# Layer-norm deviations kept on chip, another order of operand splits, and an output projection that reads its last operands last

## The chip, the cores and the metric

The kernel runs on one core of a Trainium2 chip. The metric is device time in microseconds (us), the median of several executions. Engines run in parallel and each runs its own instructions in program order: PE (matmul) with its weight loads (PEld), DVE and ACT (elementwise), POOL, and SP, which here only issues transfers. ACT and POOL issue transfers too. Semaphores hold an instruction until what it needs is there.

## What is computed

One encoder block on x of 1024 positions by 1024 channels, float32. Two mixers read the same normalised input, their gated sum goes through an output projection, and a gated MLP with a convolution follows.

```python
def conformer_conv(a, g, dw_w, dw_b, ln_g, ln_b):
    h = a * jax.nn.sigmoid(g)
    h = depthwise_conv(h, dw_w, dw_b)
    h = layer_norm(h, ln_g, ln_b)
    return jax.nn.silu(h)

n = rms_norm(h, norm1_g[l])
z = n @ w_in[l]
z_u, z_v, z_a, z_g, z_ga, z_gb = jnp.split(z, split_at, axis=-1)
y_a = spatial_gating(jax.nn.gelu(z_u), jax.nn.gelu(z_v), ...) @ w_a_out[l]
y_b = conformer_conv(z_a, z_g, ...) @ w_b_out[l]
merged = jax.nn.sigmoid(z_ga) * y_a + jax.nn.sigmoid(z_gb) * y_b
h = h + merged @ w_o[l]
n = rms_norm(h, norm2_g[l])
gate, val = jnp.split(n @ w_up[l], 2, axis=-1)
gate = depthwise_conv(gate, ffn_dw_w[l], ffn_dw_b[l])
h = h + (jax.nn.gelu(gate) * val) @ w_down[l]
out = rms_norm(h, final_g)
```

## The kernel before

Activations are held transposed, 128 channels by 1024 positions a tile (512 KB). Every operand of a matmul is split by `split` into a rounded high part (a cast by ACT) and a low part (a subtraction by DVE), and a product of two operands is three matmuls: high x high, high x low, low x high. `mm_both` does this for one output tile: for each of eight operand blocks k, six matmuls of 128 x 512, so 48 for an output.

Order of the program: the input projections (u, v, a, g, then the gates ga and gb), the products with w_a and w_b, the output projection with w_o, the MLP. While the gate projections run on PE, the layer norm of the convolution (`conv_norm`) is done in the background: `fill` takes steps off the list `bg` according to a planner's clock, `PE.now`, which adds up assumed costs. Its steps: `mean` (sum of the channels by two matmuls), eight `dev` (load a tile from DRAM, subtract the mean, store it to DRAM, square it, add the square to `csum`), `var` and `var2` (reciprocal standard deviation, broadcast), eight `fin` (load the deviations again, multiply, Silu). After each second `fin`, `c_sums` makes four sums and differences of the pair, which POOL stores to `fb_d`; from there the operands of the convolution's units are read.

The products with w_a and w_b are done by `strassen`: eight units (`ab_units`; 0 to 3 are branch A with w_a, 4 to 7 branch B with w_b), each with seven products (1 to 7) of half size, instead of eight. A unit wants weight sums. `Unit` lets POOL make them by accumulating transfers while loading; `SumUnit` loads the weights once and lets DVE add. The operand blocks of unit 0 are loaded and split by `s_blocks` and prepared in the last three gate projections (`prepare`); within a unit, `slot` after each product hands out the next splits and loads. Between two products a copy by ACT (L659, L666, L671, L676) moves a half bank; the products 1, 3, 5 and 6 among others stand behind such copies.

`Merged` fetches the merged branch (`merged_d`) in unit 7 and splits its first six tiles; the last two, from unit 7 itself, are multiplied, added and split by `direct` at its end. Then the output projection: for each output j a load of x, a weight from `W.get()` (which also splits up to two further weights ahead), 48 matmuls, `evac_o` (addition to x by DVE, a square by ACT, a sum by DVE, for each half) and a store to `h_d`.

Pools: `ap` gives 16 slots of 8 KB a partition, tag a8, to the eight normalised activations, the split operand blocks and some weights; `wp` gives 3 slots to weights; `sp` gives 15 slots of 4 KB to everything else. A tile that takes a slot waits until the last reader of the slot's tile before is through. There are four banks of the matmul's output.

## Time and profile before

| | |
|---|---|
| executions | 1505.01, 4063.05, 1500.4 us; median 1505.01 |
| profiled execution | 1502.72 us, span 1500.9 us, mean granted clock of PE 0.989 |
| PE | 1460.4 us busy, 97% |
| PEld | 1211.4 us, 81% |
| DVE | 1027.2 us, 68% |
| ACT | 630.3 us, 42% |
| POOL | 144.5 us, 10% |

A view of the trace gives either totals (the page, the waits) or rows in order of time (the timeline): where a row says "[7.70 <-ACT w L130]", its engine sat idle for 7.70 us before, until an instruction of ACT at line 130 that writes a tile w. The granted clock of PE is a share of 2.4 GHz; 0.50 is 1.2 GHz.

### The profile page before, as it was taken

Reading aid. Unit: us, or ns where it says so; the run is one execution under the profiler, and the core shown is the slowest. Engines: PE = TensorE matmul, PEld = TensorE weight load, DVE = VectorE, ACT = ScalarE, POOL = GpSimd, SP = SyncE. Lnnn points to the kernel's source line nnn. Section 1 sums busy time; section 2 is a strip of 40 time slices with the busy share of each in tenths; the row PEclk is TensorE's granted clock in tenths of the full one; section 3 lists DMA queues with packets and bytes.
Section 4 is the critical chain, followed back from the end, with each engine's and each line's share of the span. In section 5 each row is a group of like instructions: output and inputs, shape, how many; then the busy total and the mean of one; then the engine's idle time right before and its main releaser. Section 6 shows DMA issues by size and latency. Waiting matters only on the chain.

```text
span 1500.9 us, 17240 instructions
## 1 busy us (share of the span) xinstructions
PE 1460.4 (97%) x6634; PEld 1211.4 (81%) x6634; DVE 1027.2 (68%) x1085; ACT 630.3 (42%) x769; POOL 144.5 (10%) x180
## 2 busy tenths in 40 slices
PE   9999999999999996999999999999999999999998
PEld 7888888888888875878788888888888887878887
DVE  6899989888999746595644875555555448464545
ACT  6433244343422555363323454444444447363353
POOL 0000000000000011000000012111111111112000
PEclk9999999999999997999999999999999999999999
DMA  5343575445614788577444289777777779999743
GB/s 202 98 96 100 157 196 150 119 134 160 164 62 154 270 299 327 183 285 235 139 155 141 72 223 262 201 200 198 199 196 198 187 186 296 282 369 289 254 174 113
DMA packets 108770, 289.70 MB, mean 193 GB/s; under 512 B 10640, under 2 KB 12944, under 8 KB 108688
## 3 DMA queue, kind: packets, MB, share of 16 engines
q1 hardware_dynamic: 76032, 207.85, 40.0%
q0 software_dynamic: 24000, 57.68, 19.7%
q10 hardware_dynamic: 8656, 23.08, 4.0%
q8 instruction: 52, 0.85, 0.2%
q14 instruction: 30, 0.25, 0.1%
HBM read 185.80 MB, written 73.40 MB: 173 GB/s over the span
## 4 chain that ended last, share of the span: by engine, by line
PE 79%; DVE 9%; DMA 5%; issue 3%; ACT 3%; SPq 1%; ACTq 0%; DVEq 0%; POOLq 0%
PE bank L69 79%; DVE s L69 7%; DMA s<-fb_d 2%; DVE a L69 2%; DMA s<-in_w_down 1%; DMA fb_d<-s 1%; ACT a L130 1%; DMA h_d<-s 1%; DVE w L69 0%; DMA s<-in_xT 0%; DMA s<-h_d 0%; ACT w L130 0%; ACT s L792 0%; SPq L539 0%; DVE hb L69 0%
## 5 line engine op out<-in xcount | busy, mean ns | idle before, releaser
L69 PE MATMUL bank<-a,w 128*128 128x512 f32 (+1 forms) x4146 | 952.9, 389 | 24.9 <-ACT w L130 8.6
L69 PEld LDWEIGHTS bank<-a,w 128*128 128x128 f32 x4146 | 773.1, 189 | 190.6 <-ACT w L130 9.4
L69 PE MATMUL bank<-a,a 128*128 128x512 f32 (+2 forms) x1934 | 419.0, 374 | 7.1 <-ACT s L671 6.2
L69 PEld LDWEIGHTS bank<-a,a 128*128 128x128 f32 x1934 | 344.3, 189 | 73.5 <-ACT s L671 7.1
L69 DVE TENSOR_TENSOR w<-s,w 128x1024 fp32r<-128x1024 f32 (+3 forms) x144 | 162.0, 1127 | 222.9 <-ACT w L130 215.9
L69 DVE TENSOR_TENSOR a<-s,a 128x1024 fp32r<-128x1024 f32 (+2 forms) x186 | 198.5, 1093 | 134.8 <-ACT a L130 134.4
L69 DVE SCALAR_TENSOR_TENSOR s<-hb,vt,s 128x1024 f32<-128x1024 f32 x204 | 248.2, 1277 | 0.0
L130 ACT CAST w<-s 128x1024 fp32r<-128x1024 f32 (+2 forms) x143 | 138.8, 973 | 136.6 <-PE bank L69 88.2
L130 ACT CAST a<-s 128x1024 fp32r<-128x1024 f32 (+2 forms) x142 | 138.7, 996 | 66.8 <-DVE s L69 19.2
L69 DVE TENSOR_TENSOR s<-s,bank 128x1024 f32<-128x1024 f32 (+2 forms) x128 | 110.4, 881 | 36.2 <-PE bank L69 25.4
L69 DVE TENSOR_TENSOR s<-s,s 128x1024 f32<-128x1024 f32 (+1 forms) x98 | 95.4, 980 | 10.4 <-ACT s L780 7.9
L69 PE MATMUL bank<-w,a 128*128 128x512 f32 x384 | 87.2, 389 | 0.0
L69 PEld LDWEIGHTS bank<-w,a 128*128 128x128 f32 x384 | 72.1, 188 | 15.0
L586 POOL DMA_DIRECT2D s<-s x56 | 49.4, 882 | 269.5 <-DMA s<-in_w_up 87.2
L586 POOL DMA_DIRECT2D s<-in_w_up x40 | 41.1, 1028 | 266.3 <-DMA s<-in_w_up 243.9
L69 DVE TENSOR_TENSOR csum<-csum,s 128x1024 f32<-128x1024 f32 (+2 forms) x55 | 45.7, 831 | 22.4 <-ACT s L1432 11.2
L676 ACT ACTIVATE s<-bank 128x512 f32<-128x512 f32 x36 | 21.5, 598 | 93.9 <-PE bank L69 93.8
L446 POOL DMA_DIRECT2D s<-s x28 | 24.3, 866 | 371.0 <-ACT s L445 309.2
L659 ACT COPY bank<-bank 128x512 f32<-128x512 f32 x36 | 20.6, 571 | 67.2 <-PE bank L69 66.8
L671 ACT ACTIVATE s<-bank 128x512 f32<-128x512 f32 x36 | 21.5, 597 | 60.3 <-PE bank L69 57.6
L931 ACT ACTIVATE s<-bank 128x1024 f32<-128x1024 f32 x16 | 16.4, 1025 | 69.7 <-PE bank L69 62.0
L1220 ACT ACTIVATE s<-s 128x1024 f32<-128x1024 f32 x22 | 23.3, 1061 | 38.4 <-DVE s L69 38.4
(87 smaller groups left out, 562.5 us busy)
## 6 DMA issues: line engine op xcount, KB each, us to landing
s<-in_w_up SPq DMA_DIRECT2D x64, 512.0 KB, 7.0
s<-fb_d SPq DMA_DIRECT2D x50, 512.0 KB, 8.1
s<-in_w_in SPq DMA_DIRECT2D x39, 512.0 KB, 4.4
s<-s POOLq DMA_DIRECT2D x28, 512.0 KB, 6.4
s<-s POOLq DMA_DIRECT2D x56, 256.0 KB, 4.6
fb_d<-s SPq DMA_DIRECT2D x24, 512.0 KB, 2.8
s<-in_w_down SPq DMA_DIRECT2D x24, 512.0 KB, 8.1
s<-h_d SPq DMA_DIRECT2D x24, 512.0 KB, 8.3
```

What stands on the lines that cost most here:

```text
L69: return fn(*args, **kwargs)
L130: A.copy(dst_hi, src)
L446: G.dma_start(box[k % 2], p, accum_op=ALU.add)
L586: G.dma_start(r[:, 0 if i == 3 else 1], add, accum_op=ALU.add)
L659: A.copy(x[:, 1], x[:, 0])
L671: A.activation(u[:, 0], x[:, 1], AF.Copy, scale=-1.0)
L676: A.activation(u[:, 1], x[:, 1], AF.Copy, scale=-1.0)
L931: A.activation(t, ps.rearrange("p a b -> p (a b)"), AF.Sigmoid)
L1220: A.activation(t, t, AF.Gelu_apprx_tanh)
```

## The change

1. `conv_norm` keeps the deviations. Four of them are written into two new tiles of the pool a8 (a pair each), four stay in the slots into which they were loaded. The store after the subtraction and the second load go. Three loads are issued already by `mean`.
2. In the last three gate projections `prepare` comes ahead of `fill`.
3. Unit 4, the first of branch B, is a `Unit` instead of a `SumUnit`.
4. `Merged` splits a weight of the output projection after products 5 and 6 of unit 7, and not after 6 alone. The splits of the last two merged tiles are taken out of `direct` into `keep`, which comes after both `direct`.
5. The output projection takes two weights at its start, runs outputs 0 and 1 over six of the eight blocks, and then finishes each with blocks 7 and 6. Output 2 takes its weight behind the evacuations of 0 and 1.

```diff
--- before.py
+++ after.py
@@ -206,7 +206,7 @@
                     stop=last and i == n - 1 and hw == 1,
                 )
 
-    def mm_both(ps, w, rhs, ks):
+    def mm_both(ps, w, rhs, ks, first=True, last=True):
         n = len(ks)
         widened(ps)
         for i, k in enumerate(ks):
@@ -218,8 +218,8 @@
                         ps[:, half],
                         w[:, hw, k],
                         rhs(k, hx, half),
-                        start=i == 0 and (hw, hx) == (0, 0),
-                        stop=i == n - 1 and hw == 1,
+                        start=first and i == 0 and (hw, hx) == (0, 0),
+                        stop=last and i == n - 1 and hw == 1,
                     )
 
     K8 = list(range(KT))
@@ -738,6 +738,8 @@
             mu = sm()
             A.activation(mu, ps.rearrange("p a b -> p (a b)"), AF.Copy, scale=1.0 / D)
             mus["mu"] = mu
+            for j in range(3):
+                load(j)
             bg.extend(dev(j) for j in range(KT))
             bg.append(lambda: soon.extend([lambda ps: None, var]))
 
@@ -754,15 +756,17 @@
 
         def dev(j):
             def run():
-                if j == 0:
-                    load(0)
-                if j < KT - 1:
-                    load(j + 1)
-                t = mus.pop(j)
-                V.tensor_tensor(t, t, mus["mu"], op=ALU.subtract)
-                A.dma_start(conv_d[j], t)
+                if j + 3 < KT:
+                    load(j + 3)
+                t = d = mus.pop(j)
+                if j < 4:
+                    if j % 2 == 0:
+                        mus["pair"] = abig([P, 2, S], F32)
+                    d = mus["pair"][:, j % 2]
+                V.tensor_tensor(d, t, mus["mu"], op=ALU.subtract)
+                mus["dev", j] = d
                 q = mus["q", j] = sm()
-                A.activation(q, t, AF.Square)
+                A.activation(q, d, AF.Square)
                 if j > 0:
                     add(j - 1)
                 if j == KT - 1:
@@ -783,11 +787,7 @@
 
         def fin(j):
             def run():
-                if j == 0:
-                    load(0)
-                if j < KT - 1:
-                    load(j + 1)
-                t = mus.pop(j)
+                t = mus.pop(("dev", j))
                 V.tensor_tensor(t, t, mus["r"], op=ALU.mult)
                 A.activation(t, t, AF.Silu, bias=vec_ap(V_CBB, j), scale=vec_ap(V_CG, j))
                 mus["c", j] = t
@@ -953,6 +953,7 @@
 
 
     ab_units = [SumUnit(w[j : j + 2]) for w in (w_a, w_b) for j in range(0, KT, 2)]
+    ab_units[4] = Unit(w_b[0:2])
 
     def prepare(n):
         if n == 0:
@@ -998,9 +999,9 @@
         mm_both(ps, w, n_rhs, K8)
         while stores:
             stores.popleft()()
-        fill(PE.now)
         if i >= len(order) - 3:
             prepare(i - len(order) + 3)
+        fill(PE.now)
         if kind == "a":
             evac_a(ps, j)
         elif kind == "g":
@@ -1075,7 +1076,7 @@
                 mT[i] = abig([P, 2, S])
                 split(mT[i][:, 0], mT[i][:, 1], self.raw.pop(i))
                 self.load(i + 2)
-            if i == 5:
+            if i in (4, 5):
                 W.split()
                 W.issue()
 
@@ -1111,6 +1112,8 @@
         def direct(q, src):
             times(q, src)
             V.tensor_tensor(g[q], g[q], g[2 + q], op=ALU.add)
+
+        def keep(q):
             mT[j + q] = abig([P, 2, S])
             split(mT[j + q][:, 0], mT[j + q][:, 1], g[q])
 
@@ -1118,7 +1121,7 @@
         if u < 6:
             later.extend([lambda: times(0, flat(x)), lambda: times(1, flat(neg)), lambda: out(0), lambda: out(1)])
         else:
-            later.extend([lambda: direct(1, flat(neg)), lambda: direct(0, flat(x))])
+            later.extend([lambda: direct(1, flat(neg)), lambda: direct(0, flat(x)), lambda: keep(1), lambda: keep(0)])
 
     run_units(
         ab_units,
@@ -1170,12 +1173,21 @@
 
     h_d = dp.tile([KT, P, S], F32, name="h_d")
     ssums = [csum[:, 0:HALF], csum[:, HALF:S]]
+
+    ready = [W.get(ahead=1), W.get(ahead=0)]
+    early = [bank2(), bank2()]
+    for w, ps in zip(ready, early):
+        mm_both(ps, w, m_rhs, K8[:6], last=False)
     for j in range(3):
         hT[j] = sm()
         SP.dma_start(hT[j], xT[j * P : (j + 1) * P])
-        w = W.get()
-        ps = bank2()
-        mm_both(ps, w, m_rhs, [0, 1, 2, 3, 4, 5, 7, 6])
+        if j < 2:
+            ps = early[j]
+            mm_both(ps, ready[j], m_rhs, [7, 6], first=False)
+        else:
+            w = W.get()
+            ps = bank2()
+            mm_both(ps, w, m_rhs, K8)
         for half in range(2):
             evac_o(ps, j, half, ssums[half])
         SP.dma_start(h_d[j], hT[j])
```

Where this moves instructions is seen in the orders of the engines (a name such as s_3601 is a tile; "waits" lists the semaphores: PE, DVE or Activation for an engine, DMAHW for transfers issued by SP or ACT, DMASW for those issued by POOL). ACT around the last gate projection, where the first unit of branch A is prepared, before: the copy of the normalisation's factor, Silu by Silu, and then the two casts of the fourth operand block.

```order
L780 COPY s_3634<-bank_75 128x1024 [waits DMAHW4_49,DMASW6_49,PE_49]
L792 ACT_TABLE_LOAD
L792 ACTIVATE s_3674<-s_3674,vt 128x1024 [waits DVE_49]
L792 ACTIVATE s_3676<-s_3676,vt 128x1024 [waits DVE_49]
L792 ACTIVATE s_3680<-s_3680,vt 128x1024 [waits DVE_49]
L792 ACTIVATE s_3684<-s_3684,vt 128x1024 [waits DVE_49]
L792 ACTIVATE s_3694<-s_3694,vt 128x1024 [waits DMAHW1_49,DVE_49]
L792 ACTIVATE s_3698<-s_3698,vt 128x1024 [waits DVE_49]
L130 CAST a_3712<-s_3607 128x2x512 [waits DMAHW2_49]
L130 CAST a_3715<-s_3609 128x2x512 [waits DMAHW4_49]
L931 ACT_TABLE_LOAD [waits DMASW1_49,PE_49]
L931 ACTIVATE s_3720<-bank_74 128x1024 [waits Activation_49]
```

The same place now:

```order
L784 COPY s_3628<-bank_75 128x1024 [waits PE_49]
L130 CAST a_3668<-s_3601 128x2x512 [waits DMAHW2_49,PE_49]
L130 CAST a_3671<-s_3603 128x2x512 [waits DMAHW4_49,PE_49]
L792 ACT_TABLE_LOAD
L792 ACTIVATE a_3382<-a_3382,vt 128x1024 [waits DVE_49] x2
L792 ACTIVATE a_3450<-a_3450,vt 128x1024 [waits DVE_49] x2
L792 ACTIVATE s_3386<-s_3386,vt 128x1024 [waits DVE_49]
L931 ACT_TABLE_LOAD
L931 ACTIVATE s_3698<-bank_74 128x1024
L932 DMA gb_d<-s_3698 128x1024 [waits Activation_49]
L130 CAST w_3757<-s_3605 128x1024 [waits DMAHW5_49]
L130 CAST w_3763<-s_3760 128x1024 [waits DVE_49]
```

The two casts (now of a_3668 and a_3671) went from behind six Silu to ahead of the first, and have a wait for PE which they did not have; behind the Silu follow the sigmoid of the last gate but one and the casts of two weights.

DVE a little later, before: the sums of the last pair, then the splits and sums of weights.

```order
L69 TENSOR_TENSOR s_3779<-s_3779,s_3634 128x1024 [waits DMAHW7_49,DMASW2_49]
L69 TENSOR_TENSOR s_3791<-s_3779,s_3708 128x512 [waits DMASW5_49,Activation_49]
L69 SCALAR_TENSOR_TENSOR s_3791<-s_3791,s_3708 128x512 [waits DVE_49]
L69 SCALAR_TENSOR_TENSOR s_3792<-s_3791,s_3779 128x512 [waits DMASW6_49,DVE_49]
L69 TENSOR_TENSOR s_3792<-s_3708 128x512
L69 TENSOR_TENSOR w_3797<-s_3611,w_3797 128x1024 [waits PE_49,Activation_49]
L69 TENSOR_TENSOR s_3800<-s_3611,s_3718 128x512 [waits DMAHW6_49,DMASW7_49]
L69 TENSOR_TENSOR s_3800<-s_3800,s_3718 128x512 [waits DVE_49]
```

Now (the third pair's second sum is s_3771, stored by POOL, which owns DMASW3; the gate's store by ACT owns DMAHW3):

```order
L69 TENSOR_TENSOR s_3461<-s_3461,s_3628 128x1024
L69 TENSOR_TENSOR s_3817<-s_3461,s_3455 128x512 [waits DMASW3_49,Activation_49]
L69 SCALAR_TENSOR_TENSOR s_3817<-s_3817,s_3455 128x512 [waits DVE_49]
L69 SCALAR_TENSOR_TENSOR s_3818<-s_3817,s_3461 128x512 [waits DMASW2_49,DMAHW3_49,DVE_49,Activation_49]
L69 TENSOR_TENSOR s_3818<-s_3455 128x512
L69 TENSOR_TENSOR w_3823<-s_3674,w_3823 128x512 [waits PE_49,Activation_49]
L69 TENSOR_TENSOR s_3826<-s_3674 128x512 [waits DMASW5_49,DVE_49]
L69 TENSOR_TENSOR s_3826<-s_3760,s_3605 128x512
L69 TENSOR_TENSOR a_3829<-s_3785,a_3829 128x2x512 [waits DMAHW1_49,Activation_49]
```

The last pair's sums take slots whose tiles before were still to be stored, and what follows on DVE, the low part of a weight (w_3823), two sums of weights and the low part of an operand block, follows these waits.

ACT where the output projection begins, before: the cast of a weight, those of merged tiles 7 and 6, two weights, the squares of output 0 (L1143), a weight.

```order
L130 CAST w_4886<-s_4744 128x1024 [waits DMAHW6_49]
L130 CAST a_4906<-s_4761 128x1024 [waits DVE_49]
L130 CAST a_4911<-s_4759 128x1024 [waits DVE_49]
L130 CAST w_4917<-s_4889 128x1024 [waits DMAHW5_49]
L130 CAST w_4922<-s_4920 128x1024 [waits DMAHW7_49,PE_49]
L1143 ACTIVATE s_4976<-s_4915 128x512 [waits DMAHW6_49,DVE_49,Activation_49]
L1143 ACTIVATE s_4980<-s_4915 128x512 [waits DMAHW2_49,DVE_49]
L130 CAST w_4986<-s_4925 128x1024 [waits DMAHW0_49,PE_49,Activation_49]
```

Now (the squares are at L1146):

```order
L130 CAST w_4871<-s_4856 128x1024 [waits DMAHW7_49]
L130 CAST a_4893<-s_4741 128x1024 [waits DVE_49]
L130 CAST a_4896<-s_4739 128x1024 [waits DVE_49]
L1146 ACTIVATE s_4987<-s_4972 128x512 [waits DMAHW1_49,DVE_49,Activation_49]
L1146 ACTIVATE s_4991<-s_4972 128x512 [waits DMAHW4_49,DVE_49]
L1146 ACTIVATE s_5010<-s_4995 128x512 [waits DMAHW3_49,DVE_49,Activation_49]
L1146 ACTIVATE s_5014<-s_4995 128x512 [waits DVE_49,Activation_49]
L130 CAST w_5020<-s_4874 128x1024 [waits DMAHW0_49,PE_49]
L130 CAST w_5025<-s_5023 128x1024 [waits DMAHW6_49,PE_49,Activation_49]
```

The cast of the third weight, w_5020, stands behind the squares of outputs 0 and 1. SP at the same place now:

```order
L1183 DMA s_4972<-in_xT 128x1024 [waits DMAHW1_49,DVE_49]
L1193 DMA h_d<-s_4972 128x1024 [waits DMAHW2_49,DMAHW1_49,DVE_49]
L1183 DMA s_4995<-in_xT 128x1024 [waits DMAHW5_49,DMAHW3_49,Activation_49]
L1193 DMA h_d<-s_4995 128x1024 [waits DMAHW4_49,DMAHW3_49,DVE_49]
L1183 DMA s_5018<-in_xT 128x1024 [waits Activation_49]
L148 DMA s_5023<-in_w_o 128x1024 [waits DMAHW6_49,Activation_49]
L148 DMA s_5028<-in_w_o 128x1024 [waits DMAHW7_49,Activation_49]
L148 DMA s_5033<-in_w_o 128x1024 [waits DMAHW0_49]
```

The load of x for output 1 stands behind the store of output 0, as it did before; before, the loads of the weights for outputs 2 and 3 stood ahead of that store.

## Rows read from the trace of the kernel before

**Rows 1.** The page: span of the profiled execution, and busy time of each engine.
```profile
span 1500.9 us, 17240 instructions
...
PE 1460.4 (97%) x6634; PEld 1211.4 (81%) x6634; DVE 1027.2 (68%) x1085; ACT 630.3 (42%) x769; POOL 144.5 (10%) x180
```

**Rows 2.** Waits of PE: engine, line, waited for: us in total, times, longest.
```profile
PE bank L69 <- ACT s L671: 11.5, 6, 4.2
PE bank L69 <- ACT w L130: 8.6, 2, 7.7
```

**Rows 3.** Timeline of PE, first change: start us, us, operation, count [idle before, releaser].
```profile
542.34 17.97 PE L69 MATMUL bank<-a,w 128*128 128x512 f32 x78
...
568.24 1.22 PE L69 MATMUL bank<-a,w 128*128 128x512 f32 x2 [7.70 <-ACT w L130]
571.22 15.85 PE L69 MATMUL bank<-a,w 128*128 128x512 f32 x58 [1.76 <-DVE w L69]
591.25 5.49 PE L69 MATMUL bank<-a,a 128*128 128x512 f32 x12 [4.18 <-ACT s L671]
```

**Rows 4.** Timeline of PE, second and third change.
```profile
673.48 3.04 PE L69 MATMUL bank<-a,a 128*128 128x512 f32 x12 [2.04 <-ACT s L671]
...
733.58 4.49 PE L69 MATMUL bank<-a,w 128*128 128x512 f32 x12 [2.66 <-ACT s L671]
738.75 41.31 PE L69 MATMUL bank<-a,w 128*128 128x512 f32 x180 [0.69 <-ACT s L676]
```

**Rows 5.** Windows: us, busy of PE, PEld, DVE, ACT, POOL; clock, DMA share, GB/s.
```profile
568.00:570.00 2.00, 1.22 (x2) 0.50 (x2) 1.96 (x4) 0.18 (x1) 1.08 (x2) 0.50 1.08 387
```

**Rows 6.** Timeline of ACT and DVE around the first change.
```profile
542.62 1.02 ACT L780 COPY s<-bank 128x1024 f32<-128x1024 f32 x1 [4.74 <-PE bank L69]
543.65 1.28 ACT L792 ACT_TABLE_LOAD   x1
543.67 3.50 DVE L69 TENSOR_TENSOR s<-s,s 128x1024 f32<-128x1024 f32 x3 [7.89 <-ACT s L780]
544.95 3.51 ACT L792 ACTIVATE s<-s,vt 128x1024 f32<-128x1024 f32 x3
...
548.09 1.42 DVE L69 SCALAR_TENSOR_TENSOR s<-s,s 128x512 f32<-128x512 f32 x2
...
557.63 1.98 ACT L130 CAST a<-s 128x1024 fp32r<-128x1024 f32 x2
...
558.69 2.36 DVE L69 TENSOR_TENSOR a<-s,a 128x1024 fp32r<-128x1024 f32 x2 [2.25 <-ACT a L130]
...
567.16 1.03 ACT L130 CAST w<-s 128x1024 fp32r<-128x1024 f32 x1
...
576.30 0.57 ACT L659 COPY bank<-bank 128x512 f32<-128x512 f32 x1 [0.40 <-ACT s L931]
```

**Rows 7.** Transfers around the first change: landings of fb_d, stores of gb_d, the chain's.
```profile
DMA to landing us min/median/max: 2.7/7.8/13.4
...
gb_d<-s ACTq DMA_DIRECT2D x2, 512.0 KB, 7.3
...
583.87 5.77 DMA s<-fb_d
```

**Rows 8.** Timeline of DVE, ACT and SP's queue, output projection.
```profile
753.80 0.68 DVE L69 TENSOR_TENSOR s<-s,bank 128x512 f32<-128x512 f32 x1
...
756.70 0.38 SPq L1175 DMA_DIRECT2D s<-in_xT  x1
...
763.78 0.69 DVE L69 TENSOR_TENSOR s<-s,bank 128x512 f32<-128x512 f32 x1 [4.67 <-PE bank L69]
...
767.03 1.03 ACT L130 CAST a<-s 128x1024 fp32r<-128x1024 f32 x1
...
777.83 0.38 SPq L1185 DMA_DIRECT2D s<-in_xT  x1
...
782.45 0.69 DVE L69 TENSOR_TENSOR s<-s,bank 128x512 f32<-128x512 f32 x1 [2.20 <-DMA s<-in_xT]
```

## The prediction

> **What bounds the kernel now.** I read the page first: the profiled execution took 1502.72 us, its span is 1500.9 us [rows 1], so 1.8 us lie outside it, and the execution stands 2.3 us under the median of 1505.01. PE is busy 1460.4 us of the span. What can be won is therefore PE's idle time, some 40 us, and what its clock loses after each pause. The waits of PE say who ends that time: most of it is ACT, whose copies and casts of operands come late [rows 2]. PE's timeline shows where: almost all of the idle time that this change can touch lies in three places where one matmul group hands over to the next. At the first change of operands (gate projections to the convolution unit's seven products) PE stops for 7.70, 1.76 and 4.18 us [rows 3]; at the second (branch A to branch B) for 2.04 us; at the third (branch B to the output projection) for 2.66 and 0.69 us [rows 4]. Last the windows: after a pause PE runs at a granted clock of 0.50, that is at 1.2 instead of 2.4 GHz [rows 5]. So 12 matmuls take 5.49 us behind the pause of 4.18 us, 4.49 us behind that of 2.66 us, and 3.04 us behind that of 2.04 us [rows 3, 4]; at the pace of the 78 matmuls before the first change (17.97 / 78 = 0.230 us each) they take 2.76 us. The three places together cost 7.70 + 1.76 + 4.18 + 2.04 + 2.66 + 0.69 = 19.0 us of pauses and some 9 us of clock.
>
> **The change, part by part.**
>
> *Deviations on chip.* Eight stores and eight loads of 512 KB go away. Both lie in stretches in which PE is never out of work, so what they free is worth nothing by itself. The issues that ACT loses are short (a queue entry takes 0.38 us on SP [rows 8]) and lie in the same stretch. What counts is where the deviations now live. Four of them sit in two tiles of the pool that also holds the operands: its 16 slots hold 8 normalised activations, 6 split blocks of the first unit, and 2 pairs. The order of ACT shows what follows: the casts of the fourth block, which before waited only for their own loads and stood behind six Silu, now stand ahead of all eight Silu and wait for PE, because their slots are those of the first two activations, read last in the last gate product. Behind a waiting cast ACT stands still: Silu, sigmoid, and the first weight's cast.
>
> I follow this chain from the end of the last gate product at 542.34 + 17.97 = 560.31. Its last 48 matmuls begin at 560.31 - 48 x 0.230 = 549.2; the first activation is done with after six (550.6), the second after twelve (552.0). Prices are those of [rows 6]: cast 0.99, low part 1.18, table load 1.28, multiplication 1.17, Silu 1.17, sums of a pair 4 x 0.71 = 2.8, copy or sigmoid of a whole bank 1.02, weight cast 1.03; a store's issue 0.38 [rows 8]. Casts end at 551.7 and 553.1, low parts at 554.4. The multiplications that began at 543.67 now begin at 554.4, 10.7 us later. Three of them end at 557.9, the first pair's sums at 560.8, two more multiplications at 563.1. ACT: fifth Silu 564.3, table 565.6, sigmoid 566.6, issue of its store 567.0, weight cast 568.0. So product 1 starts at 568.1, where it starts at 568.24 now: the first pause stays. The low part of that weight ends at 569.2 (now 571.22 [rows 3]), 1.9 us earlier. DVE goes on with the second weight (573.0), two multiplications (575.4), the third pair's sums (578.2), the last multiplication (579.4); ACT with the last Silu (580.5), table (581.8), sigmoid (582.8), and, behind its store's issue, with the copy of a bank that product 3 waits for, which ends at 583.8 instead of 576.87 [rows 6].
>
> Then two new waits of DVE, in the order of its rows: the last pair's first sum waits for a store by POOL of the third pair, its last sums also for ACT's store of the gate. The first is issued at 578.2 + 0.7 = 578.9 and lands 7.8 us later, by the median of the part tiles (2.7 to 13.4 [rows 7]): 586.7; two sums end at 588.1. The second is issued at 583.2 and lands 7.3 us later [rows 7], at 590.5. Two sums, a weight's low part and two sums of the fourth weight, at about 0.7 each: 594.0. The sixth block's load stands behind them on SP: + 5.8 us [rows 7] = 599.8, its cast 600.8, the copy of a bank (0.57) 601.4. Product 6 starts there, now at 591.25: 10.2 us later. The clock gives some back: the 12 matmuls after 591.25 now lose 5.49 - 2.76 = 2.7 us, while in the new order the slow matmuls are those of product 5, which ends inside the wait; I take the whole 2.8 (the pause in front of product 6 is shorter then). **+7.4 us.**
>
> A rule bears on the largest unknown here. The Trainium skill, page "DMA: Bandwidth & Descriptors", section "Anatomy of one DMA — SWDGE (gpsimd) path", gives a transfer about 2.0 us plus its bytes over 436 GB/s, which for 512 KB is an estimate of 3.2 us. The trace differs: its median is 7.8 us [rows 7]. By the rule the two landings that decide product 6 (7.3 and 5.8 above) would take 3.2 each, it would start at 594.7, x would land 1.4 us sooner, and the whole change would come out near 1510; I go by the rows, which were measured in this stretch.
>
> *Splits before fill.* One part of the same order; it is what moves the casts ahead of the Silu, and is in the sum above. Were the slots free it would cost nothing: two casts of 0.99 us on ACT, which sat idle for 4.74 us ahead of 542.62 [rows 6].
>
> *Second change: Unit in place of SumUnit.* Four sums of 0.68 us by DVE go, four 256 KB accumulations by POOL come, and SP issues four loads instead of two. The pause there is 2.04 us and ends with a copy by ACT [rows 4]. What DVE no longer does sits ahead of that copy, but only in part: between 0 and 4 x 0.68 = 2.7 us, at most the pause and its clock. I take one sum, **-0.7 us**. The accumulations must be through before POOL's additions to the merged branch; POOL is busy 144.5 us in all [rows 1], so they hide. If they were late, the load waits for them, a landing of 7.8 us against a lead of two products; that is in R2.
>
> *Third change.* Now the pauses there cost 2.66 + 0.69 + (4.49 - 2.76) = 5.1 us. In the new order blocks 7 and 6 of the merged branch are read last, after 72 matmuls over blocks 0 to 5 (two outputs of 36), and the splits of those two, though later than now, end some 8 us ahead of their use: 5.1 goes down to the 0.69 that the last unit's copy holds. That gain is real: **-4.4 us.** But only two output weights are ready, and two is what the two early products use. The third weight's cast stands on ACT behind four squares of outputs 0 and 1; output 1 needs its rows of x; that load stands on SP behind output 0's store, which waits for output 0's evacuation. From the end E of output 0's products: addition begins E + 0.2; from that to the issue of the next x, 756.70 - 753.80 = 2.9; landing 782.45 - 777.83 = 4.6: E + 7.7. From output 1's addition to the next cast 767.03 - 763.78 = 3.25; cast 1.03 and low part 1.2 [rows 6, 8]: E + 13.2. PE has 12 matmuls meanwhile (2.8 us). It stands still for 9.3 us before the high part and 0.7 more between the parts: 10.0 us. A pause that long costs clock after it as well: behind 7.70 us two matmuls took 1.22 us and the next 58 took 15.85 [rows 3], 17.07 - 60 x 0.230 = 3.3; behind 4.18 it was 2.7. I take 3.1. **+13.1, net +8.7 us.** In the order of before the weights are fetched one output ahead, and each output's 48 matmuls (11 us) cover the same chain.
>
> Sum: 7.4 - 0.7 + 8.7 = +15.4; 1502.72 + 15.4 = **1518.1 us**.
>
> **Rivals.**
>
> R1, transfers land sooner: 8.4 MB less to move makes the landings ahead of product 6 as short as the shortest, 2.7 us [rows 7]. Then the gate's store is through at 583.2 + 2.7 = 585.9, the sums and low part behind it end at 589.4, the load lands at 592.1, cast and copy end at 593.7. With the clock's gain that is -0.3 at the first change; with x landing 1.9 us sooner the third costs +6.8; with -0.7: +5.8, **1508.5**. For it: fewer bytes. Against: the load that remains is the blocks', and the same queue's transfers differ by five times in one stretch.
>
> R2, they land late, 13.4 us each [rows 7]: the gate's store at 596.6, sums 600.1, load 613.5, product 6 at 615.1, which is 23.9 late, less 2.8 of clock: +21.1 - 0.7 + 8.7 = +29.1, **1531.8**. It decides once that store and that load take over 27.8 us together, where the forecast has 13.1. For it: 13.4 us is a landing of that tile in this very stretch. Against: it is the longest there.
>
> R3, on the other side: the change does what its parts say. Casts find their slots free and the third weight is there in time. Then the pauses go: 7.70 + 1.76 + 4.18 and 6.3 of clock at the first, 2.04 at the second, 5.1 at the third: -27, **1475.7**, 1.8% faster. Against: both waits stand in the orders of ACT and SP; it would need the first two activations to be free by 542, 8 us before PE reads them last. With the first change free and the third weight late it would be 1502.7 - 19.9 - 0.7 + 8.7 = 1490.8.
>
> **How the numbers follow.** Forecast 0.76, R1 0.14, R2 0.05, R3 and its half 0.05. The likeliest gives 1518.0. Its unknowns are the landings (2.7 to 13.4 each), the clock behind 10 us of pause (2.7 to 3.5) and the second change (0 to 2.7); all rarely lie at one end. The range from 1506 to 1527 takes in R1 and the half of the way to R2 and leaves out R3 and R2, about 2 in 10. About 2% (30 us) is what a measurement of this kernel can tell from no change: slower needs over 1535, beyond R2's 1531.8; faster needs under 1475, below R3. So within 2% has 0.95, slower 0.03, faster 0.02.
>
> **What would show it.** Right: the two casts of the fourth block wait for PE until about 551 and 552, with no Silu before 554; a pause of about 7.5 us before product 1; a copy of a bank at 583 instead of 576; product 6 near 601 with a pause of some 10 us ahead of it; no pause over 1 us at the last unit's end, and a new one of 9 to 10 us, at a clock of 0.50 behind it, before the third output's first matmul, ended by ACT's cast of a weight. Wrong: the Silu run from 544 as now (then the slots were free), or the third weight's cast stands before the squares; or the landings ahead of product 6 are near 3 us.

## The result

The changed kernel takes 1524.03 us (four runs, 1523.04 to 1525.09), the kernel before 1503.62; the ratio is 1.0143, 95% interval 1.0121 to 1.0165. So it is some 21 us slower, where 1518 was forecast, in a range from 1506 to 1527. Its profiled execution took 1523.04 us with a span of 1521.3, 20.4 more than before [rows 1].

The page of the changed kernel (span, busy time of the engines, transfers):

```profile
span 1521.3 us, 17229 instructions
...
PE 1467.4 (96%) x6634; PEld 1216.4 (80%) x6634; DVE 1024.7 (67%) x1081; ACT 631.2 (41%) x769; POOL 148.1 (10%) x184
...
DMA packets 107714, 283.15 MB, mean 186 GB/s; under 512 B 10480, under 2 KB 12784, under 8 KB 107632
```

PE does the same 6634 matmuls. It was busy 7.0 us longer, which is clock (0.982 granted on average, 0.989 before), and idle 13.4 us longer. The waits of PE name who ended that time (us in total, times, longest):

```profile
PE bank L69 <- ACT w L130: 17.1, 3, 8.8
PE bank L69 <- ACT bank L659: 7.4, 1, 7.4
PE bank L69 <- ACT s L676: 6.2, 4, 2.7
PE bank L69 <- ACT s L671: 5.4, 4, 2.0
PE bank L69 <- DVE a L69: 5.0, 4, 4.0
```

Against [rows 2], the casts of weights cost 17.1 us and not 8.6, and the copy at L659, which cost nothing before, 7.4. The timeline of PE shows where, at the three changes of operands:

```profile
569.78 8.42 PE L69 MATMUL bank<-a,w 128*128 128x512 f32 x24 [7.66 <-ACT w L130]
585.63 7.36 PE L69 MATMUL bank<-a,w 128*128 128x512 f32 x25 [7.43 <-ACT bank L659]
596.97 5.06 PE L69 MATMUL bank<-a,w 128*128 128x512 f32 x11 [3.98 <-DVE a L69]
603.89 3.02 PE L69 MATMUL bank<-a,a 128*128 128x512 f32 x12 [1.85 <-ACT s L671]
...
669.10 12.84 PE L69 MATMUL bank<-a,w 128*128 128x512 f32 x48 [2.12 <-ACT s L676]
...
686.02 3.06 PE L69 MATMUL bank<-a,a 128*128 128x512 f32 x12 [1.37 <-ACT s L671]
...
746.89 24.77 PE L69 MATMUL bank<-a,w 128*128 128x512 f32 x108 [0.69 <-ACT s L676]
780.46 19.51 PE L69 MATMUL bank<-a,w 128*128 128x512 f32 x72 [8.80 <-ACT w L130]
```

To compare kernels I cut the span at four points of this timeline that all of them have: the matmul of the layer norm's variance (533.39 before, 534.97 after), the end of the first 12 matmuls of product 6 in unit 0 (596.74; 606.91), the group of matmuls that the 0.69 us pause precedes (738.75; 746.89), and the first matmul of the second norm (812.55; 832.45). The stretches between them are the first, second and third change. "Before" holds its old pause of the third change (2.66 us and slow matmuls, 4.4 in all) in the second stretch; in the table I moved it to the third.

| stretch | before | after | difference | forecast |
|---|---|---|---|---|
| up to the variance | 533.39 | 534.97 | +1.6 | 0 |
| first change | 63.35 | 71.94 | +8.6 | +7.4 |
| second change | 137.6 | 139.98 | +2.4 | -0.7 |
| third change | 78.2 | 85.56 | +7.4 | +8.7 |

The rest of the 20.4 us, 0.5, lies behind. ACT and DVE at the first change show how the forecast's chain runs (subtract 1.6 us to compare with the forecast's times):

```profile
544.20 1.02 ACT L784 COPY s<-bank 128x1024 f32<-128x1024 f32 x1 [4.74 <-PE bank L69]
552.40 1.05 ACT L130 CAST a<-s 128x1024 fp32r<-128x1024 f32 x1 [7.18 <-PE bank L69]
...
553.76 1.05 ACT L130 CAST a<-s 128x1024 fp32r<-128x1024 f32 x1 [0.30 <-PE bank L69]
554.83 1.28 ACT L792 ACT_TABLE_LOAD   x1
555.99 3.49 DVE L69 TENSOR_TENSOR a<-a,s 128x1024 f32<-128x1024 f32 x3
...
585.01 0.57 ACT L659 COPY bank<-bank 128x512 f32<-128x512 f32 x1 [0.41 <-ACT s L931]
...
588.61 0.69 DVE L69 TENSOR_TENSOR s<-s,s 128x512 f32<-128x512 f32 x1 [7.62 <-DMA fb_d<-s]
...
592.68 0.69 DVE L69 SCALAR_TENSOR_TENSOR s<-s,s 128x512 f32<-128x512 f32 x1 [2.66 <-DMA gb_d<-s]
```

ACT stands still for 7.18 us until PE has read the first activation; the multiplications begin at 555.99, where [rows 6] has them at 543.67; the copy ahead of product 3 comes at 585.01 instead of 576.30; and DVE waits twice for a store.

### The profile page after: what moved, and what is told of

Same layout as the page of the kernel before. It is cut to its first block, busy times and chain, and to the rows that moved or that the text cites. A ratio compares the mean times of both kernels' runs of the same rounds, so it can differ in the third digit from the quotient of the medians.

```text
span 1521.3 us, 17229 instructions
## 1 busy us (share of the span) xinstructions
PE 1467.4 (96%) x6634; PEld 1216.4 (80%) x6634; DVE 1024.7 (67%) x1081; ACT 631.2 (41%) x769; POOL 148.1 (10%) x184
## 4 chain that ended last, share of the span: by engine, by line
PE 77%; DVE 7%; issue 7%; DMA 6%; ACT 2%; POOL 1%; SPq 0%; ACTq 0%; DVEq 0%; POOLq 0%
PE bank L69 77%; DVE s L69 6%; DMA s<-fb_d 2%; DMA s<-h_d 1%; DVE a L69 1%; DMA s<-in_xT 1%; DMA fb_d<-s 1%; DMA s<-in_w_down 1%; ACT a L130 1%; DVE w L69 0%; POOL fb_d L516 0%; ACT w L130 0%; DVE hb L69 0%; ACT s L931 0%; ACT s L671 0%
## 5 line engine op out<-in xcount | busy, mean ns | idle before, releaser
L69 PE MATMUL bank<-a,w 128*128 128x512 f32 (+1 forms) x4146 | 962.0, 392 | 41.0 <-ACT w L130 17.1
L69 DVE TENSOR_TENSOR s<-s,s 128x1024 f32<-128x1024 f32 (+1 forms) x85 | 82.6, 976 | 8.6 <-DMA fb_d<-s 7.6
L676 ACT ACTIVATE s<-bank 128x512 f32<-128x512 f32 x36 | 21.5, 598 | 90.0 <-PE bank L69 90.0
L659 ACT COPY bank<-bank 128x512 f32<-128x512 f32 x36 | 20.6, 571 | 67.1 <-PE bank L69 66.7
L671 ACT ACTIVATE s<-bank 128x512 f32<-128x512 f32 x36 | 21.5, 597 | 60.5 <-PE bank L69 59.5
```

What stands on the lines that cost most here:

```text
L69: return fn(*args, **kwargs)
L659: A.copy(x[:, 1], x[:, 0])
L671: A.activation(u[:, 0], x[:, 1], AF.Copy, scale=-1.0)
L676: A.activation(u[:, 1], x[:, 1], AF.Copy, scale=-1.0)
```

## The experiments

The runs change the changed kernel in one place, unless said otherwise. Ratios are to the kernel before on the same chip, with 95% intervals.

**The first change: slots or order.** Run e1 puts `fill` ahead of `prepare` again:

```diff
+        fill(PE.now)
         if i >= len(order) - 3:
             prepare(i - len(order) + 3)
-        fill(PE.now)
```

> The changed kernel with one part undone: in the last gate projections the background steps come ahead of the splits of the first unit again; the deviations stay on chip. My theory (casts wait for PE because their slots are the first two activations', and all Silu stand behind them): the casts come behind six Silu, at a time at which the activations have been read, so their wait costs nothing; multiplications start near 545 and not 556, product 6 of unit 0 starts near 593 and not 603.9, and the time is about 8.5 us below the changed kernel's 1524: 1515. Rival (the deviations' place alone does it, by the slots that are full): the pause stays wherever the casts stand, and the time stays near 1524. Rival (landings of stores decide): in between, product 6 near 598.

Run e2 has the layer norm of before and keeps the new order:

```diff
...
-                mus["dev", j] = d
+                A.dma_start(conv_d[j], t)
...
-                t = mus.pop(("dev", j))
+                if j == 0:
+                    load(0)
+                if j < KT - 1:
+                    load(j + 1)
+                t = mus.pop(j)
```

> The changed kernel with the layer norm of the convolution as before (deviations stored and loaded again), but the splits still ahead of the background steps. My theory: two slots are free, so the two casts run at once, near 545, and cost ACT and DVE some 2 to 3 us ahead of the multiplications, which they cost later anyway; product 6 near 594, time 7 to 8 us below the changed kernel's: 1516.5. Rival (the order alone does the harm): time near 1524. Rival (eight loads come back on the queue that loads the blocks, and land late): over 1520.

Run e5 keeps order and layer norm, but only the four deviations that take no slot of the operands' pool; the others are stored and loaded:

```diff
-                if j < 4:
-                    if j % 2 == 0:
-                        mus["pair"] = abig([P, 2, S], F32)
-                    d = mus["pair"][:, j % 2]
                 V.tensor_tensor(d, t, mus["mu"], op=ALU.subtract)
-                mus["dev", j] = d
+                if j < 4:
+                    A.dma_start(conv_d[j], d)
+                else:
+                    mus["dev", j] = d
...
```

> The changed kernel, order of splits included, but only four of the eight deviations are kept (the four in slots of the small pool); the first four are stored and loaded again, so that no pair takes slots of the operands' pool and the two casts find free slots. My theory (the full slots do the harm): the casts run near 545, the first change costs about what the run with the old layer norm cost, product 6 of unit 0 starts 3 to 4 us later than before by the distance from the norm's matmul, not 9 to 10, and the time is 5 to 7 us below the changed kernel's. Rival (keeping deviations at all, or the order by itself, costs the 9 us): product 6 as in the changed kernel, 68.9 us behind the norm's matmul.

Run e10 is the kernel before with the deviations on chip and nothing else.

> The kernel before with one part of the change alone: the deviations stay on chip. Order of splits, unit 4 and output projection are those of before. My theory (eight stores and eight loads lie where PE is never out of work, so they free nothing by themselves; the casts' wait for PE costs nothing behind six Silu): within 1.5 us of before, 0 to 1.5 us faster. Rival (the full slots cost wherever the casts stand): 5 us or more slower. Rival (8.4 MB less of transfers speed up the landings at the first change): 3 us or more faster.

| kernel | order | pairs in the pool | first change | ratio |
|---|---|---|---|---|
| before | old | no | 63.35 | 1 |
| e10 | old | yes | 61.88 | 0.9995 (0.9984 to 1.0005) |
| e1 | old | yes | 62.56 | 1.0037 (1.0025 to 1.0049) |
| e2 | new | no | 66.68 | 1.0083 (1.0065 to 1.0101) |
| e5 | new | no | 64.73 | 1.0082 (1.0067 to 1.0098) |
| after | new | yes | 71.94 | 1.0143 (1.0121 to 1.0165) |

The stretches are read from one profile each, the ratios from all runs; where the ratios differ more (e1 took 1509.59 us, and 1515 was expected), part of it lies outside the stretch: e1 starts the variance's matmul 2.4 us earlier than the changed kernel and loses 1.2 us less at the third change. The pairs alone cost nothing, the new order alone 1.4 to 3.3 us, both together 8.6: it is the meeting of full slots and casts that come early. The clock behind the pauses blurs these stretches. The start of product 6, counted from the variance's matmul, is free of what follows it, and falls into three groups: 57.1 to 57.9 us in the five kernels with the old order (before, e1, e8, e10, e11), 61.7 and 62.5 with the new order and free slots (e5, e2), and 68.8 to 70.3 in the seven with both (after, e3, e4, e6, e7, e9, e12). In e5, with the order of the changed kernel and free slots, ACT casts at once:

```profile
543.35 2.00 ACT L130 CAST a<-s 128x1024 fp32r<-128x1024 f32 x2
...
546.71 3.49 DVE L69 TENSOR_TENSOR s<-s,s 128x1024 f32<-128x1024 f32 x3
...
560.52 0.73 PE L69 MATMUL bank<-a,w 128*128 128x512 f32 x2 [0.15 <-ACT w L130]
```

and in e1 the casts come behind six Silu, later than PE's last reading of the two activations, and wait for nothing:

```profile
556.82 1.98 ACT L130 CAST a<-s 128x1024 fp32r<-128x1024 f32 x2
```

Product 1 of e5 starts without a pause, and yet e5 gains nothing on before: its first weight casts are early, but the copy ahead of product 3, behind the last three Silu, is late by 8.34 us instead, as in e2:

```profile
576.35 7.40 PE L69 MATMUL bank<-a,w 128*128 128x512 f32 x25 [8.34 <-ACT bank L659]
```

**The second change.** Run e3 leaves out the line `ab_units[4] = Unit(w_b[0:2])`.

> The changed kernel with unit 4 a SumUnit again (sums by DVE, two loads of 512 KB). My theory (POOL's accumulations and the two additional loads fill the DMA engines between 655 and 670, so that the blocks of branch B land at 8.5 us instead of 7, and the copy ahead of the product at 669 stands behind their casts): the pause of 2.12 us there becomes 0.4 or less, that of 1.37 grows to about 2.0 as before, and the time falls by 2.5 us to 1521.5. Rival (the pause comes from the later position in the stream of loads, or from the queue of SP): it stays at 2.1, and the time at 1524.

Its second stretch is 137.09 us, with pauses of 0.41, 0.20 and 1.35 us, against 139.98; the ratio is 1.0123 (1.0099 to 1.0146). The stretches differ by 2.9 us, and expected was that the last pause grows to 2.0 us again, which it did not. The whole time does not settle what the Unit costs, as the intervals of the two ratios overlap; nor does the stretch alone, which is 140.04 us in e8, also with the SumUnit. The pause ahead of the product behind L676 does: it is 1.5 to 2.5 us in all six kernels with the Unit (after, e1, e2, e4, e5, e7) and at most 0.20 in the five that have the SumUnit and no other transfers (before, e3, e8, e10, e11). All pauses of the stretch together are 3.5 to 5.4 us in the six and 2.0 to 3.1 in the five (without the old pause of the third change). In the changed kernel the copy at L676 stands behind two casts of branch B's blocks, whose loads were issued from 657.62 and whose casts began at 666.19 and 667.51; in e3 issue was at 657.90 and the casts at 663.75 and 665.27. The landings are late by some 2.5 us, not the issue. Is that the Unit's bytes? Run e6 has e3's SumUnit and spare transfers, which nobody reads:

```diff
...
+    class TrafficUnit(SumUnit):
+        def load(self, i):
+            if i < 2:
+                SumUnit.load(self, i)
+            elif i == 2:
+                SP.dma_start(scratch_d[:, 0 : 2 * HALF], self.src[0].rearrange("p k c -> p (k c)"))
+                G.dma_start(scratch_d[:, 2 * HALF : 3 * HALF], self.block(0, 1))
+            else:
+                SP.dma_start(scratch_d[:, 3 * HALF : 4 * HALF], self.block(1, 0))
+                G.dma_start(scratch_d[:, 4 * HALF : 5 * HALF], self.block(0, 0))
-    ab_units[4] = Unit(w_b[0:2])
+    ab_units[4] = TrafficUnit(w_b[0:2])
```

> The changed kernel with unit 4 a SumUnit again, and beside it, at the places where a Unit issues its third and fourth load, transfers of the same size from the weights into a spare tensor in DRAM, which nobody reads: SP 512 and 256 KB, POOL 256 KB twice. They take no slot of the pools, and no sum waits for them. My theory (bytes on the full DMA engines delay the blocks of branch B): the pause ahead of the product near 669 is back, 1.5 to 2.5 us, where the run with SumUnit alone has 0.2. Rival (what delays the blocks is the slot that a load of blocks must wait for until POOL's accumulation is through): no such pause, at most 0.5 us.

No pause came ahead of the product near 669 (the first of unit 4), though the stretch is 140.05 us all the same (the 12 matmuls behind its last pause took 4.60 us instead of e3's 3.01, of which more below, and that pause, with one at L666, was 1.1 us longer than in e3). But POOL, with nothing to wait for, had issued its two transfers at 593.6 and 594.2, and not where a Unit has them: only SP's two were in place, at 643 and 644, and these alone do no harm at the copy. In e9 POOL's transfers add to the rows that SP has just written and so wait for them.

> As the run with traffic, which issued POOL's spare transfers at once (near 594) and not where a Unit has them: now POOL's two transfers add to the spare rows that SP has just written, so that they wait for SP's transfer to land and come near 655, right ahead of the loads of branch B's blocks, as in a Unit. Unit 4 is a SumUnit, and no slot and no sum hangs on them. My theory (POOL's accumulations on the DMA engines at that moment delay the blocks): the loads issued near 660 land in 8 us and more instead of 6, and the copy ahead of the product near 669 is late: a pause of 1.5 to 2.5 us there. Rival (it is not the transfers but what a Unit makes wait, slots and casts of its own): pause of 0.5 us at most, as in the run with SumUnit alone.

They came at 652.03 and 652.65, 5.0 and 4.4 us ahead of the first load of blocks (657.03; in the changed kernel 656.07 and 656.79 against 657.62), and the pause was 1.06 us, between the two theories (ratio 1.0106, 1.0089 to 1.0123). In e12 a short addition to the same rows goes ahead of them and makes them later:

```diff
+                G.dma_start(scratch_d[:, HALF : HALF + 64], self.block(0, 1)[:, 0:64], accum_op=ALU.add)
                 G.dma_start(scratch_d[:, HALF : 2 * HALF], self.block(0, 1), accum_op=ALU.add)
```

> As the run with late traffic, where POOL's two spare transfers were issued 4.4 to 5 us ahead of the loads of branch B's blocks, against 0.8 to 1.6 us in a Unit. A short addition to the same spare rows goes ahead of them, which they must wait for, so that they come some 3 us later, right ahead of the loads. My theory (transfers that are on the DMA engines just then cost the landing): the pause ahead of the product near 667 grows from 1.06 to 1.5 to 2.5 us, that of a Unit. Rival (the rest of a Unit's pause comes from its own casts and waits): it stays near 1 us or falls.

The timeline of e12 (POOL's and SP's issues, casts, copy, product):

```profile
657.62 0.82 POOL L964 DMA_DIRECT2D scratch_d<-in_w_b  x1 [3.29 <-DMA scratch_d<-in_w_b]
657.71 1.46 SPq L539 DMA_DIRECT2D s<-fb_d  x2
658.19 1.11 POOL L967 DMA_DIRECT2D scratch_d<-in_w_b  x1
...
664.82 1.05 ACT L130 CAST a<-s 128x1024 fp32r<-128x1024 f32 x1 [1.75 <-DMA s<-fb_d]
...
667.40 1.05 ACT L130 CAST a<-s 128x1024 fp32r<-128x1024 f32 x1 [1.53 <-DMA s<-fb_d]
...
668.36 0.59 ACT L676 ACTIVATE s<-bank 128x512 f32<-128x512 f32 x1
...
669.00 12.78 PE L69 MATMUL bank<-a,w 128*128 128x512 f32 x48 [2.52 <-ACT s L676]
```

A pause of 2.52 us (ratio 1.0124, 1.0105 to 1.0143): with a SumUnit, transfers of POOL that no engine waits for bring the Unit's pause ahead of this product back, if they are issued beside the loads of the blocks, half of it 5 us earlier, and none where SP's stand alone. The time from the issue of the two loads to the cast of the second block, behind which the copy stands, rises with the pause, but for the last two:

| | before | e8 | e6 | e3 | e9 | e12 | after |
|---|---|---|---|---|---|---|---|
| issue to second cast, us | 6.9 | 7.2 | 7.2 | 7.4 | 8.2 | 9.7 | 9.9 |
| pause at L676, us | 0 | 0 | 0 | 0.20 | 1.06 | 2.52 | 2.12 |

So it is the transfers, and their moment. Three things stay open. The ratios of e3, e6, e9 and e12 have overlapping intervals, so the whole kernel does not show what the pause costs. e12 has no pause ahead of product 6 of unit 4, where the changed kernel has 1.37 us, so that all its pauses in the stretch are 2.9 us, no more than with a SumUnit alone. And in e9 and e12 the transfers both add and come late: no run has plain ones of POOL at that moment.

**The third change.** Run e4 changes one number.

```diff
-    ready = [W.get(ahead=1), W.get(ahead=0)]
+    ready = [W.get(ahead=1), W.get(ahead=1)]
```

> The changed kernel with one number changed: the second weight taken at the start of the output projection splits one weight ahead, so that the third weight's cast stands ahead of the squares of outputs 0 and 1. My theory: the pause of 8.80 us ahead of output 2 and the 3.0 us that the clock loses behind it both go, nothing takes their place over 1 us, and the time falls by 11 to 12 us to 1512.5. Rival (the third weight waits for its slot, until PE has read the first weight, or for its load): the pause shrinks only to 4 or 6 us and the time falls by less than 7. Rival (the fourth weight is late instead): a new pause ahead of output 3, of 3 us or more.

The pause is gone with all that followed, and the 180 matmuls run through:

```profile
747.53 41.09 PE L69 MATMUL bank<-a,w 128*128 128x512 f32 x180 [0.69 <-ACT s L676]
```

The third stretch is 73.60 us instead of 85.56, 12.0 less; the ratio is 1.0032 (1.0019 to 1.0045). The whole time fell by more, to 1509.47 us where 1512.5 was expected; that part lies outside the stretch. Neither rival shows: the slot was free, and the fourth weight in time. Run e7 shortens the chain at its middle link, the load of x:

```diff
     for j in range(3):
-        hT[j] = sm()
-        SP.dma_start(hT[j], xT[j * P : (j + 1) * P])
+        if j == 0:
+            for q in range(2):
+                hT[q] = sm()
+                SP.dma_start(hT[q], xT[q * P : (q + 1) * P])
+        elif j == 2:
+            hT[j] = sm()
+            SP.dma_start(hT[j], xT[j * P : (j + 1) * P])
```

> The changed kernel with one move: the rows of x for output 1 are loaded together with those of output 0, ahead of the store of output 0. My theory of the third change (a chain: evacuation of output 0, load of x, evacuation of output 1, cast of the third weight): without the load the chain is some 4.5 us shorter, the pause falls from 8.8 to 4 to 5 us, still ended by ACT's cast of a weight, and the time by about 4.5 us. Rival (the cast waits for the slot of the third weight, or for its load, not for the squares ahead of it): the pause stays at 8.8 us.

```profile
774.79 1.03 ACT L130 CAST w<-s 128x1024 fp32r<-128x1024 f32 x1
...
775.87 9.38 PE L69 MATMUL bank<-a,w 128*128 128x512 f32 x34 [5.23 <-ACT w L130]
```

The pause falls by 3.57 us to 5.23, a little less than expected (4 to 5 us of pause), and is still ended by the cast; the stretch falls by 5.1 us to 80.48 (ratio 1.0100, 1.0086 to 1.0114). The other 1.5 us are clock, and not an effect of the shorter pause: the 72 matmuls behind it took 17.99 us instead of 19.51, but also 18.02 in e1 and 17.97 in e6, behind pauses of 9.12 and 9.03. The chain stands.

**What is left of the change.** Run e8 mends all three: e1, e3 and e4 together. Run e11 is the kernel before with the third part alone, mended as in e4.

> The changed kernel with three parts mended: background steps ahead of the splits, unit 4 a SumUnit, and the third weight split ahead of the squares. What stays of the change: deviations on chip, the later splits of the last two merged tiles, the output projection that reads them last. By the sum of the parts measured so far against before (first change -0.8, second -0.5, third -4.6 us) the time is about 6 us under that of before: 0.996 of it. Rival (what is won at the third change depends on what the parts before it lose): within 1 us of before.

> The kernel before with the third part of the change alone, mended: the last two merged tiles are split later and read last, and the third weight is split ahead of the squares. My theory: the pause of 2.66 us and the slow 12 matmuls behind it go, no new pause over 1 us comes, 4 to 5 us under before (0.997 of it). Rival (what is won there is lost at a later pause, as outputs follow each other sooner): within 1 us of before.

e8 has 0.9968 (0.9957 to 0.9979), e11 0.9971 (0.9959 to 0.9983): both faster than before, by some 4.5 us (0.3%), and the difference between them is the deviations' part, nothing that can be measured (e10). Expected were 6 us for e8. Its profile shows 2.4 us more than before in the second stretch, most of it in unit 4, whose code is that of before: the last pause is the 2.04 us of before, but the 12 matmuls behind it took 4.56 us instead of 3.04 [rows 4], and a pause of 0.62 us at L666 is new.

## Why the prediction was right

**First change, +7.4 forecast, +8.6 measured.** The step held link by link. Less the 1.6 us by which this execution was late already, the casts waited until 550.8 and 552.2 (forecast 550.6 and 552.0), product 1 started at 568.2 (568.1), the copy ahead of product 3 at 583.4 (583.2), the last pair's first sum waited for POOL's store until 587.0 (586.7) and its last for the gate's until 591.1 (590.5), and product 6 started at 602.3 (601.4). The landings made the 0.9 us: the gate's store took 592.68 - 584.62 = 8.1 us and not 7.3, and the sixth block's load, issued with its pair from 594.05, was cast at 602.29. What I put wrongly is where PE stands still: not for 10 us ahead of product 6, but for 7.43 ahead of product 3, 3.98 behind the first matmul of 5 and 1.85 ahead of 6. The rest is clock: 2.8 were to come back, and with the matmuls of product 6 2.5 did (12 in 3.02 us, 5.49 before). That was luck: of the seven kernels with these instructions in three these 12 took 3.02 to 3.04 us (after, e7, e9), and in the four others 4.60 to 4.62 (e3, e4, e6, e12), so that the stretch is 71.9 to 74.9 us and the loss 8.6 to 11.6. Products 1, 3 and 5 were each slow in their turn (24 in 8.42, 25 in 7.36, 11 in 5.06 us), but ended inside the waits and did not move product 6. R3's condition, slots free, is e5: it would not have brought 19.9 us, since the copy ahead of product 3 then stands behind the last Silu (a pause of 8.34 us). Some of the prediction's sums are off by little: the clock's part in its first paragraph is 8.0 us by its own rows, not some 9, and in R3 6.0 at the first change, not 6.3; and R2's bound of 27.8 us lies above R2's own two landings, 26.8.

The Trainium skill, page "DMA: Bandwidth & Descriptors", section "Anatomy of one DMA — SWDGE (gpsimd) path", gives about 2.0 us plus bytes over 436 GB/s for a transfer that POOL issues, an estimate of 3.2 us for 512 KB. The prediction applied it to a store of ACT and a load of SP, which are not on the path that this section fits. The store and the load that decided here took 8 us, and R1, which went by the shortest landing, fell with them. No run here shows 3.2 us as a usual landing in this stretch.

**Second change, -0.7 forecast, +2.4 measured.** This step failed, in sign. "The accumulations must be through before POOL's additions to the merged branch ... so they hide" asked only who waits for POOL, and not which loads are under way beside its transfers: the loads of branch B's blocks land later, and the copy behind their casts with them (e3, e9, e12). And the gain of 0.7 us, from the sums that DVE no longer makes, shows in no run: the last pause of the stretch is 1.37 us in the changed kernel instead of 2.04, but 2.00 to 2.05 in the five other kernels with the Unit, and 1.35 in e3, where DVE makes the sums. Of the 2.4 us, one profile against one, the sign is what the pauses of all kernels bear out; the size is not sure. R2 named late landings, but at the first change.

**Third change, +8.7 forecast, +7.4 measured.** Both terms were right in kind. The gain was -4.4, as worked out: e11 shows it without its loss (4.4 us, 2.6 to 6.2 by its interval). The new pause was forecast at 10.0 us plus 3.1 of clock, and is 8.80 plus 3.0 (72 matmuls in 19.51 us, 16.6 at 0.230). The pause repeats, 8.71 to 9.12 us in all eight kernels that have the chain whole; the clock does not, 1.4 to 3.0 us, so that its 3.1 was in part luck. SP and ACT in the changed kernel:

```profile
768.98 0.69 DVE L69 TENSOR_TENSOR s<-s,bank 128x512 f32<-128x512 f32 x1 [11.56 <-PE bank L69]
...
771.90 0.37 SPq L1183 DMA_DIRECT2D s<-in_xT  x1
...
776.03 0.69 DVE L69 TENSOR_TENSOR s<-s,bank 128x512 f32<-128x512 f32 x1 [3.46 <-DMA s<-in_xT]
...
779.38 1.03 ACT L130 CAST w<-s 128x1024 fp32r<-128x1024 f32 x1
```

From the first addition the load of x is issued after 2.92 us (2.9), lands after 4.1 (4.6), and the cast follows after 3.35 (3.25). The 0.7 us between the weight's parts did not show as a pause: PE's granted clock was 0.50 from 780 to 786 us, and its first four matmuls, which read the high part alone, took longer than the 1.2 us of the low part's subtraction.

**Not in the forecast:** 1.6 us ahead of the variance. They are no part of the change: in the kernel's first 35 us, 94 matmuls took 23.20 us here and 21.61 before, at a clock of 0.50 from 12 to 14 us, where before had 1.00; e2 and e10 show the same (23.19 and 23.21 us), and e1, with the same code there as the changed kernel, 21.61.

The chances: within 2% held. The total was 20.4 against 15.4. The three parts were wrong by +1.2, +3.1 and -1.3 us, so that the errors partly cancelled, and 2.1 us of the difference lie in none of them.

## What to carry to other kernels

A tile that is kept on chip takes a slot, and the next tile of that slot brings its wait to the engine that writes it: see what is queued there behind it, and whether the slot's last reader is done by then. Transfers off the critical path are not free while loads on it are under way; move them or look at the landing times of their neighbours. When work is reordered so that two outputs share a start, count the operands that are ready: one weight too few cost here nearly three times what the reordering won (12.0 against 4.4 us).

## What the runs showed of the hardware

The same pause is followed by either clock. Ahead of product 6 of unit 4, where 2.0 us of idle time end with the copy at L671, the 12 matmuls behind it took 3.01 to 3.04 us in before, e1, e2, e4 and e7, and 4.56 to 4.62 us in e5, e6, e8, e9, e10 and e11 (granted clock from 673 to 675 us: 1.00 in before, 0.50 in e8). Four of the first group (e1, e2, e4, e7) had a pause of 0.8 to 1.7 us at L666 one product earlier, those of the second at most 0.6; but before, of the first group, had none there, so this does not settle it. The cause of these 1.6 us is not shown, and with them two profiles can differ by more than a part of the change is worth.

The windows of the changed kernel (us; PE, PEld, DVE, ACT, POOL busy; clock, DMA share, GB/s) show the DMA engines full while the blocks land late:

```profile
655.00:658.00 3.00, 3.00 (x15) 2.46 (x14) 3.00 (x4) 2.92 (x4) 1.76 (x2) 1.00 1.03 410
658.00:661.00 3.00, 3.00 (x15) 2.49 (x14) 3.00 (x4) 2.38 (x4) 0.00 (x0) 1.00 1.05 362
```

In the kernel before, the same stretches lie 10 us earlier (645 to 648 and 648 to 651) and moved 139 and 281 GB/s, at shares of 0.42 and 0.85. But full engines are not the whole of it: e12, with the longest pause, had 0.82 and 0.91 from 655 to 661 us. What in POOL's transfers holds the loads up is not shown.
